# A mixing layer's output gate computed by tokens with seven half products, multiplied into the normalised mLSTM rows ahead of their transposes

## The chip, the cores and the metric

The kernel runs on one core of a Trainium2 chip. Its engines are TensorE (PE in the profile, with its weight loads listed apart as PEld), VectorE (DVE), ScalarE (ACT), GpSimd (POOL) and SyncE (SP, which here only issues DMAs). Each engine works through its own list of instructions in order and waits on semaphores for the others. The metric is device time of one execution in microseconds; the execution under the profiler has a time of its own.

## The reference

One decoder layer on 512 tokens of width 1024, all in float32. One RMS-normalised input `h` goes through one wide projection, of which this case touches two pieces of 1024 columns: `v_ml`, the values of the mLSTM (4 heads of 256), and `o_ml`, its output gate.

```python
h = rmsnorm(x, norm_mix_g[i])
proj = h @ w_in[i]
qk_ml, v_ml, o_ml, if_pre, q_sw, k_sw, v_sw, g_a, g_b = jnp.split(proj, split_idx, axis=-1)
...
h_ml = mlstm_chunkwise(q_ml, k_ml, v_ml.reshape(B, S, ML_HEADS, ML_DV), ig, lf)
h_ml = h_ml * lax.rsqrt(jnp.mean(h_ml * h_ml, axis=-1, keepdims=True) + EPS)
h_ml = h_ml.reshape(B, S, ML_V_W).astype(x.dtype) * mlstm_norm_g[i].astype(x.dtype)
y_a = jax.nn.sigmoid(o_ml) * h_ml
...
merged = jax.nn.sigmoid(g_a) * (y_a @ w_branch_a[i]) + jax.nn.sigmoid(g_b) * (y_b @ w_branch_b[i])
x = x + merged @ w_out[i]
```

`ig` and `lf` are an input gate and a log forget gate of each token and head (from `if_pre`), and `y_b` is sliding-window attention. An MLP, a gated embedding and a last norm follow; the change leaves them alone.

## The kernel before

A float32 product is made of three matmuls of a rounded kind: each operand is split into a high part (a cast, on ACT) and a low part (operand less high part, on DVE), and high·high, high·low and low·high are added in PSUM. `split` (lines 131 to 138) does it, `load_w` splits a weight tile of 128x1024, `pairs` lists the three. In the profile a weight's parts are `wh` and `wl`, those of the normalised input `h`. A tile of 128 by 512 results with the contraction over 1024 takes 24 matmuls of 512 columns.

The work in order: norm and transposes of the input; the values and gates of the attention (`vs`, `gt`); its keys (`kk`, `kl`, line 357 on); the output gate `w_o`; the mLSTM's scalar gates; the values `w_vml`; the branch gates `w_gb`, `w_ga`; the projections of queries and keys mixed with the attention; then, head by head, the mLSTM's rows beside the projection `w_b`; `w_a`; `w_out`; the MLP and the rest.

The output gate before. `o_proj(i)` computes eight tiles of 128 channels by 512 tokens (`proj_T`, the channels on the partitions), takes a sigmoid on ACT, and stores the tile in DRAM (`god`) by a DMA that POOL issues. Its eight calls are spread: two after the scalar gates' work, three after the sums of `h` (below), three after the transposes of the scalar gates. Much later `ya_of(h)` transposes the normalised rows of head `h`, multiplies them by the norm's gain and by the gate loaded back from `god` (line 825, tile `sy`), and splits the result into `ya`.

The values before. `vml` uses a scheme of seven half products in place of eight: tokens, contraction and columns are each cut in halves, and `seven` (line 488) forms sums of weight blocks on DVE (lines 497, 498, 503, 505) and products with parts of `h` and with sums `S1` to `S4` of parts of `h`. The sums `s1` to `s4` (line 449) and their splits (`hS`) are made once and serve the branch gates too. Each half product is 24 matmuls of 512 columns, four weight tiles' worth of two, and each goes to a pair of PSUM banks: X for `p1` and then `c11`, Z for `t21`, `t22`, `c12`, Y for `c22`, `c21`. `p1` is copied out of X by ACT (line 548) before the second product is added onto X; `t21` and `t22` are read out of Z by DVE (line 553) before the next product is added onto Z.

What sets the order. The kernel is written as one stream; a scheduling layer lays out a list for each engine, close to the written order with some instructions pulled ahead, and it may not change the order of two that depend on each other. `tc.issue_after` names an instruction behind which others must stand. Tiles come from pools with a fixed number of buffers: four each for `wh`, `wl` and raw weights `wr`, four `lm`, two `pT`, 34 of 128x512 (`act`), and in PSUM two each of `g`, `t` (one bank) and `a` (two banks).

Of the kernel before, what the change touches and what calls it, by code (L numbers as in the profile page):

```python
# [10 lines left out]
F32 = mybir.dt.float32  # L11
F32R = mybir.dt.float32r
AF = mybir.ActivationFunctionType
# [10 lines left out]
NH = 4  # L24
# [12 lines left out]
def block_kernel(  # L37
# [309 lines left out]
    def proj_T(wd, i, bank=ps_g):  # L347
        ps = bank()
        mm_T(ps, load_w(wd[i], KT * P, KT), hT)
        return ps  # L350
# [15 lines left out]
        kk.append(both)  # L366
        kl.append(low)


    dp = pool(ctx, "dp", space=bass.MemoryType.DRAM)  # L370
    god = [dp.tile([P, 2, 512], F32, name=nm("god")) for _ in range(4)]


    obanks = []

    def o_bank(i):
        if i in (0, 1, 6, 7):
            return ps_g()
        if i == 2:
            obanks.extend(four_a())  # L380
        return obanks[i - 2]

    def o_proj(i):
        ps = proj_T(w_o, i, lambda: o_bank(i))
        t = act_f("sgo")
        A.activation(t, ps, AF.Sigmoid)
        nc.gpsimd.dma_start(out=god[i // 2][:, i % 2, :], in_=t)


    pgi, pgf = ps_t(), ps_t()  # L390
    for m in range(NT):
        T.transpose(pgi[:4, m * P : (m + 1) * P], gt[:, m, :4], ident)
# [8 lines left out]
    A.activation(lf, lf, AF.Ln, bias=1.0)  # L401
    V.scalar_tensor_tensor(lf, fg, 0.0, lf, ALU.min, ALU.subtract)
    mst = act_f("mst")[:4, :]
    V.tensor_tensor_scan(mst, lf, ig, 0.0, ALU.add, ALU.max)
    fl = act_f("fl")[:4, :]
    for c in range(NT):
        V.tensor_tensor_scan(fl[:, c * P : (c + 1) * P], lf[:, c * P : (c + 1) * P], zeros4, 0.0, ALU.add, ALU.add)
    rr = act_f("rr")[:4, :]
    V.tensor_sub(rr, fl, mst)
# [12 lines left out]
    em = act_f("em")[:4, :]  # L422
    A.activation(em, mst, AF.Exp, scale=-1.0)
    o_proj(0)
    o_proj(1)


    hf[0] = tk("hf")[:, :D].rearrange("p (k c) -> p k c", k=KT)
# [37 lines left out]
    S3 = h_split(s3)  # L466
    S4 = h_split(s4)
# [20 lines left out]
    def seven(form, prod, X, Y, Z, b, post):  # L488


        b11, b12, b21, b22 = b
        n = range(len(b11))
        for i in n:
            prod(X, A11, form(b11[i]), i, True)
        post("p1", X)
        for i in n:
            V.tensor_sub(b12[i], b22[i], b12[i])
            V.tensor_add(b11[i], b12[i], b11[i])
        for i in n:
            prod(X, A12, form(b21[i]), i, False, True)  # L500
        post("c11", X)
        for i in n:
            V.tensor_sub(b21[i], b21[i], b11[i])
            prod(Z, S2, form(b11[i]), i, True)
            V.tensor_sub(b11[i], b22[i], b11[i])
        post("t21", Z)
        for i in n:
            prod(Z, S1, form(b11[i]), i, False)
        post("t22", Z)
        for i in n:  # L510
            prod(Y, S3, form(b12[i]), i, True)
        post("c22", Y)
        for i in n:
            prod(Z, S4, form(b22[i]), i, False, True)
        post("c12", Z)
        for i in n:
            prod(Y, A22, form(b21[i]), i, False, True)
        post("c21", Y)
# [5 lines left out]
        G.memset(t[:, :, DV : DV + 1], 1.0)  # L524
        vm.append(t)

    def vml():
        raws = quads(w_vml, ["wr", "wr", "lm", "lm", "wr", "wr", "lm", "lm"])
        a, b = ps_a(), ps_a()
        X, Y, Z = [a[:, :512], a[:, 512:]], [b[:, :512], b[:, 512:]], [ps_g(), ps_g()]  # L530
        keep = {}

        def prod(ps, f, w, kh, first, last=False):
            for t in range(2):
                ops = []
                for k in range(2):
                    ops += pairs([h[:, t * P : (t + 1) * P] for h in f[2 * kh + k]], [h[:, k, :] for h in w])
                chain(ps[t], ops, first and kh == 0, last and kh == 1, True)

        def post(what, ps):  # L540
            for t in range(2):
                if what[0] == "c":
                    half, nh = int(what[1]), int(what[2]) - 1
                    o = vm[t + (2 if half == 1 else 0)][:, 2 * nh : 2 * nh + 2, :DV]
                    src = ps[t].rearrange("p (h d) -> p h d", h=2)
                if what == "p1":
                    keep["p1", t] = act_f("p1")
                    A.copy(keep["p1", t], ps[t])
                elif what == "c11":
                    A.copy(o, src)  # L550
                elif what[0] == "t":
                    keep[what, t] = act_f(what)
                    V.tensor_add(keep[what, t], ps[t], keep["p1", t])
                else:
                    k = keep["p1" if what == "c12" else "t" + what[1:], t]
                    V.tensor_add(o, src, k.rearrange("p (h d) -> p h d", h=2))

        seven(lambda r: load_w(None, 1024, 2, r), prod, X, Y, Z, [raws[2 * i : 2 * i + 2] for i in range(4)], post)

    vml()  # L560

# [237 lines left out]
    def ml_norm(heads, rds):  # L799
        n = len(heads) * NT  # L800
        rs = rstd_of(hss[:, heads[0] : heads[-1] + 1, :].rearrange("p h t -> p (h t)"), DV)
        for j, h in enumerate(heads):
            V.tensor_mul(rs[:, j * NT : (j + 1) * NT], rs[:, j * NT : (j + 1) * NT], rds[j])
            for t in range(NT):
                V.tensor_scalar_mul(h_of(h, t), h_of(h, t), rs[:, j * NT + t : j * NT + t + 1])


    t2 = [None] * 8
# [9 lines left out]

    def ya_of(h):
        for i in (2 * h, 2 * h + 1):  # L820
            sg = act_f("sy")
            pt = ps_t()
            for t in range(NT):
                T.transpose(pt[:, t * P : (t + 1) * P], h_of(h, t)[:, (i % 2) * P : (i % 2 + 1) * P], ident)
            V.scalar_tensor_tensor(sg, pt, gml[:, i : i + 1], gate_of(god, i), ALU.mult, ALU.mult)
            split(ya[i], sg)

    ml_weights(0)
    rds = []
# [352 lines left out]
    return w.reshape(2, 2, 2, P, 2, 512).transpose(0, 2, 4, 3, 1, 5).reshape(8, P, 1024)  # L1182


def _heads(w):

    k = w.shape[0]
    return w.reshape(k, 2, 2, 4, 64).transpose(0, 1, 3, 2, 4).reshape(k, 1024)
# [6 lines left out]
def _layout(i):  # L1195
# [3 lines left out]
        "x": i["x"][0],  # L1199
        "p": i["p"][0, 0],  # L1200
        "w_qkml": _t_form(w[:, 0:1024]),
        "w_vml": _quarters(w[:, 1024:2048]).reshape(2, 4, P, 1024).transpose(1, 0, 2, 3).reshape(8, P, 1024),
# [41 lines left out]
```

## Time and profile before

| | |
|---|---|
| median of 3 runs | 906.15 us (904.98 to 906.18) |
| the profiled execution's own time | 905.84 us |
| its span, first to last instruction | 904.1 us |
| PE, DVE, ACT busy in the span | 890.4, 627.0, 466.9 us |
| from the first `w_o` matmul's stretch to the first branch gate's | 38.96 to 123.42 us |

A row of a time list reads: start, duration, engine, line, operation, out<-in, shapes, count, and in brackets the idle time of the engine before it and who ended it. Consecutive instructions of an engine overlap by their latency, so the cost of one in a row of many is the distance of starts. A row of waits reads: who waited, for whom, total us, times, longest. In a table by stretches each engine's busy time stands with its count of instructions.

### The profile page before, as it was taken

How to read it: one execution, taken by the hardware profiler on the slowest of the kernel's cores; microseconds unless marked ns; L12 is line 12 of the kernel's file. 1: busy time of each engine (PE TensorE's matmuls, PEld its weight loads, DVE VectorE, ACT ScalarE, POOL GpSimd, SP SyncE). 2: the span in 40 equal slices, each digit the busy share in tenths (PEclk: the TensorE clock that was granted, in tenths of full speed). 3: DMA queues.
4: the chain of work that ended last, by engine and by line, in shares of the span. 5: the costliest groups of instructions: out<-in, count | busy, mean ns of one | idle time of the engine just before them, and what ended most of it. 6: DMA issues, size and time to landing. Idle time of an engine off the chain costs nothing.

```text
span 904.1 us, 11781 instructions
## 1 busy us (share of the span) xinstructions
PE 890.4 (98%) x4500; PEld 741.6 (82%) x4500; DVE 627.0 (69%) x1016; ACT 466.9 (52%) x778; POOL 28.1 (3%) x47
## 2 busy tenths in 40 slices
PE   8999999999999999999999999999999999999996
PEld 7888899998877677777878888888888888888786
DVE  6884687874787977557644568856965795689556
ACT  6473444443676667664322555345535543554753
POOL 2021000000000000001210000000000000000000
PEclk9999999999999999999999999999999999999999
DMA  7753134435121132234452620631262044101402
GB/s 259 252 159 125 47 116 157 149 122 168 61 70 52 43 117 71 94 103 150 144 187 94 228 74 2 209 119 45 68 212 94 1 162 161 49 24 50 160 1 94
DMA packets 30347, 101.52 MB, mean 112 GB/s; under 512 B 4301, under 2 KB 4813, under 8 KB 30290
## 3 DMA queue, kind: packets, MB, share of 16 engines
q1 hardware_dynamic: 28002, 93.15, 31.0%
q0 software_dynamic: 2144, 7.35, 2.3%
q8 instruction: 35, 0.57, 0.3%
q10 hardware_dynamic: 144, 0.26, 0.1%
q14 instruction: 22, 0.18, 0.1%
HBM read 91.30 MB, written 8.40 MB: 110 GB/s over the span
## 4 chain that ended last, share of the span: by engine, by line
PE 73%; ACT 2%; DVE 2%; DMA 1%; issue 0%; SPq 0%; ACTq 0%
PE psg L162 42%; PE psp L162 22%; PE pst L784 2%; PE pst L713 1%; PE psa L705 1%; PE pst L774 1%; PE psa L162 1%; PE psa L668 1%; PE psa L669 1%; DMA gfin<-in_g_fin 1%; PE psp L877 1%; ACT jk L796 1%; ACT wh L134 1%; ACT pT L707 0%; DMA ptok<-in_p 0%
## 5 line engine op out<-in xcount | busy, mean ns | idle before, releaser
L135 DVE TENSOR_TENSOR wl<-wr,wh 128x1024 fp32r<-128x1024 f32 x134 | 170.7, 1279 | 131.0 <-ACT wh L134 124.4
L134 ACT CAST wh<-wr 128x1024 fp32r<-128x1024 f32 x134 | 140.9, 1053 | 208.5 <-PE psg L162 85.6
L162 PE MATMUL psg<-x,wh 128*128 128x512 f32 x512 | 157.9, 389 | 0.0
L162 PE MATMUL psp<-wh,uf 128*128 128x512 f32 x448 | 139.2, 390 | 0.0
L162 PEld LDWEIGHTS psg<-x,wh 128*128 128x128 f32 x512 | 96.0, 188 | 19.8
L162 PE MATMUL psg<-h,wh 128*128 128x512 f32 x320 | 101.3, 395 | 0.0
L162 PE MATMUL psg<-x,wl 128*128 128x512 f32 x256 | 99.6, 389 | 0.0
L162 PEld LDWEIGHTS psp<-wh,uf 128*128 128x128 f32 x448 | 84.1, 188 | 17.4
L162 PE MATMUL psp<-wl,uf 128*128 128x512 f32 x224 | 87.2, 390 | 0.0
L134 ACT CAST wh<-wd 128x1024 fp32r<-128x1024 f32 x44 | 46.3, 1055 | 60.4 <-PE psp L162 23.2
L162 PEld LDWEIGHTS psg<-h,wh 128*128 128x128 f32 x320 | 58.7, 188 | 15.9 <-issue 4.9
L135 DVE TENSOR_TENSOR wl<-wd,wh 128x1024 fp32r<-128x1024 f32 x44 | 53.3, 1220 | 17.6 <-ACT wh L134 17.4
L162 PE MATMUL psg<-h,wl 128*128 128x512 f32 x160 | 62.8, 393 | 0.0
L162 PEld LDWEIGHTS psg<-x,wl 128*128 128x128 f32 x256 | 48.1, 188 | 10.0
L162 PE MATMUL psa<-h,wh 128*128 128x256 f32 (+1 forms) x256 | 55.1, 311 | 0.2 <-ACT p L593 0.2
L162 PEld LDWEIGHTS psp<-wl,uf 128*128 128x128 f32 x224 | 42.0, 188 | 8.7
L135 DVE TENSOR_TENSOR uf<-F,uf 128x1792 fp32r<-128x1792 f32 (+2 forms) x20 | 33.0, 1652 | 21.8 <-ACT uf L134 21.8
L162 PEld LDWEIGHTS psa<-h,wh 128*128 128x128 f32 x256 | 41.8, 190 | 3.7 <-ACT p L593 0.9
L162 PE MATMUL psg<-yb,wh 128*128 128x512 f32 x128 | 42.7, 408 | 0.0
L162 PE MATMUL psg<-ya,wh 128*128 128x512 f32 x128 | 40.7, 394 | 0.0
L162 PE MATMUL psa<-h,wl 128*128 128x256 f32 (+1 forms) x128 | 39.6, 309 | 0.0
L134 ACT CAST uf<-F 128x1792 fp32r<-128x1792 f32 (+2 forms) x20 | 28.0, 1399 | 19.3 <-DVE F L951 19.2
(284 smaller groups left out, 1667.7 us busy)
## 6 DMA issues: line engine op xcount, KB each, us to landing
wr<-in_w_up SPq DMA_DIRECT2D x32, 512.0 KB, 3.2
wd<-in_w_down SPq DMA_DIRECT2D x24, 512.0 KB, 3.3
wr<-in_w_o SPq DMA_DIRECT2D x8, 512.0 KB, 4.8
gd<-gr POOLq DMA_DIRECT2D x8, 512.0 KB, 3.2
wr<-in_w_qsw SPq DMA_DIRECT2D x8, 512.0 KB, 4.0
wr<-in_w_qkml SPq DMA_DIRECT2D x8, 512.0 KB, 3.3
wr<-in_w_b SPq DMA_DIRECT2D x8, 512.0 KB, 3.2
gl<-gd SPq DMA_DIRECT2D x8, 512.0 KB, 3.4
```

Of the source, the lines that this page charges most:

```text
L134: A.copy(dst[0], src)
L135: V.tensor_sub(dst[1], src, r32(dst[0]))
L162: last_mm[0] = T.matmul(ps, l, r, start=first and i == 0, stop=last and i == len(ops) - 1, skip_group_check=parts)
L668: T.matmul(o, q[:, n * P : (n + 1) * P], kk[kp][ab][:, k0 : k0 + 256], start=True, stop=False)
L669: T.matmul(o, q[:, n * P : (n + 1) * P], kl[kp][ab][:, k0 : k0 + 256], start=False, stop=True)
L705: T.transpose(pt[:, c : c + P], lm3[ab][:, g, j * P : (j + 1) * P], ident)
L713: T.matmul(o[HALF[ab], :], vs[n + 1 - nk + j][:, c : c + 64], pTs[j][:, ab * 512 : (ab + 1) * 512], start=j == 0, stop=j == nk - 1,)
L774: T.matmul(psc[:, n0:], qk[4 + h][:, n0 : n0 + P], qk[h][:, n0:], start=True, stop=True)
L784: T.matmul(pn[:, : DV + 1], wT[s][:, t * P : (t + 1) * P], vm[s][:, h, :], start=s == 0, stop=s == t)
L796: A.activation(jk[:, :DV], h_of(h, t), AF.Square, scale=rd[:, t : t + 1], accum_out=hss[:, h, t : t + 1])
L877: T.transpose(ps[:, m * P : (m + 1) * P], xk[m][:, k * P : (k + 1) * P], ident)
```

## The change

The output gate is computed by tokens (tokens on the partitions), with `seven`, as the values are, and through the same code: `by_tokens(w, post)` is the old `vml`, and `post_by_tokens(done)` its old `post`. `w_vml` is computed first, directly behind the keys; the scalar gates' work follows; then `w_o`. The weights of `w_o` are laid out as those of `w_vml`. The gate's quarter results go through a sigmoid (`put_o`) to one DRAM tile `god` of tokens by heads. `ml_norm` loads a head's gate (`og`) and multiplies it into the normalised rows in the instruction that scaled them; `ya_of` transposes these rows and splits them, with the gain as scale, straight out of PSUM. The definitions and the work of `s1` to `s4` move ahead of the scalar gates. In the values' call alone the third product is placed behind the second (`own_first`).

```diff
-    def o_proj(i):
-        ps = proj_T(w_o, i, lambda: o_bank(i))
-        t = act_f("sgo")
-        A.activation(t, ps, AF.Sigmoid)
-        nc.gpsimd.dma_start(out=god[i // 2][:, i % 2, :], in_=t)
...
+    s1, s1h = h_sum("s1", hf_part(2, 1), hf_part(2, 2), ALU.add)
+    s2, s2h = h_sum("s2", s1h, hf_part(1, 1), ALU.subtract)
+    S2 = h_split(s2)
+    S1 = h_split(s1)
+    s4, _ = h_sum("s4", hf_part(1, 2), s2h, ALU.subtract)
+    s3, _ = h_sum("s3", hf_part(1, 1), hf_part(2, 1), ALU.subtract)
+    S3 = h_split(s3)
+    S4 = h_split(s4)
+
+    def seven(form, prod, X, Y, Z, b, post, own_first=False):
...
+        for i in n:
+            prod(X, A11, form(b11[i]), i, True)
+        post("p1", X)
+        for i in n:
+            V.tensor_sub(b12[i], b22[i], b12[i])
+            V.tensor_add(b11[i], b12[i], b11[i])
+        for i in n:
+            prod(X, A12, form(b21[i]), i, False, True)
+        own = last_mm[0].ins
+        post("c11", X)
+        for i in n:
+            V.tensor_sub(b21[i], b21[i], b11[i])
+            w = form(b11[i])
+            with tc.issue_after(own) if own_first else ExitStack():
+                prod(Z, S2, w, i, True)
+            V.tensor_sub(b11[i], b22[i], b11[i])
...
+    def post_by_tokens(done):
+
+        keep = {}
+
+        def post(what, ps):
+            for t in range(2):
+                if what == "p1":
+                    keep["p1", t] = act_f("p1")
+                    A.copy(keep["p1", t], ps[t])
+                elif what[0] == "t":
+                    keep[what, t] = act_f(what)
+                    V.tensor_add(keep[what, t], ps[t], keep["p1", t])
+                else:
+                    k = None if what == "c11" else keep["p1" if what == "c12" else "t" + what[1:], t]
+                    done(t + (2 if what[1] == "1" else 0), int(what[2]) - 1, ps[t], k)
...
+    by_tokens(w_vml, post_by_tokens(put_v), True)
 
     pgi, pgf = ps_t(), ps_t()
...
-    o_proj(0)
-    o_proj(1)
...
-    for i in range(2, 5):
-        o_proj(i)
...
-    for i in range(5, 8):
-        o_proj(i)
...
-    vml()
+    god = dp.tile([P, NH, NT, DV], F32, name="god")
+
+    def put_o(m, nh, ps, k):
+        if k is None:
+            k = act_f("sgo")
+            A.activation(k, ps, AF.Sigmoid)
+        else:
+            V.tensor_add(k, ps, k)
+            A.activation(k, k, AF.Sigmoid)
+        nc.gpsimd.dma_start(out=god[:, 2 * nh : 2 * nh + 2, m, :], in_=k.rearrange("p (h d) -> p h d", h=2))
+
+    by_tokens(w_o, post_by_tokens(put_o))
...
+            og = tok_scratch("og").rearrange("p (t d) -> p t d", t=NT)
+            nc.sync.dma_start(out=og, in_=god[:, h])
             for t in range(NT):
-                V.tensor_scalar_mul(h_of(h, t), h_of(h, t), rs[:, j * NT + t : j * NT + t + 1])
+                c = j * NT + t
+                V.scalar_tensor_tensor(h_of(h, t), h_of(h, t), rs[:, c : c + 1], og[:, t, :], ALU.mult, ALU.mult)
...
-            V.scalar_tensor_tensor(sg, pt, gml[:, i : i + 1], gate_of(god, i), ALU.mult, ALU.mult)
-            split(ya[i], sg)
+            split(ya[i], pt, gml[:, i : i + 1])
...
-        "w_o": _t_form(w[:, 2048:3072]),
+        "w_vml": _by_quarter(w[:, 1024:2048]),
+        "w_o": _by_quarter(w[:, 2048:3072]),
```

The first place is ACT where the values' first product is copied out. Before, at the start of `vml`, the casts of the sums (`hS`) lie far back, behind the first tiles of the output gate, and the copies stand between casts of weights:

```order
L386 ACTIVATE sgo_147_819<-psg_143_788 128x512
L134 CAST wh_177_940<-wr_162_874 128x1024
L386 ACTIVATE sgo_152_853<-psg_148_822 128x512
L134 CAST wh_179_959<-wr_157_864 128x1024
L548 COPY p1_173_916<-psa_165_880 128x512
L548 COPY p1_174_918<-psa_165_880 128x512
L134 CAST wh_181_977<-wr_158_866 128x1024
```

The same place in the change, ACT again; `psa_105` is X, `wh_119` and `wh_121` are weights of the third product, the names from `hS_75` to `hS_91` the high parts of `s2`, `s1`, `s3`, `s4`:

```order
L134 CAST wh_119_613<-wr_97_518 128x1024
L134 CAST hS_75_472<-s2_74_469 128x512
L134 CAST hS_77_476<-s2_74_469 128x512
L134 CAST wh_121_631<-wr_98_520 128x1024
L134 CAST hS_79_480<-s1_73_466 128x512
L134 CAST hS_81_484<-s1_73_466 128x512
L134 CAST hS_85_494<-s3_84_491 128x512
L134 CAST hS_87_498<-s3_84_491 128x512
L134 CAST hS_89_502<-s4_83_488 128x512
L134 CAST hS_91_506<-s4_83_488 128x512
L479 COPY p1_113_570<-psa_105_534 128x512
L479 COPY p1_114_572<-psa_105_534 128x512
```

All eight casts of the sums now stand ahead of the two copies of `p1`.

The second place is DVE, which makes the sums that those casts read. Before, `s4` and `s3` are made right behind the splits of `s2` and `s1`, with one weight's low part among them:

```order
L135 TENSOR_TENSOR hS_107_596<-s2_105_592,hS_106_595 128x512
L135 TENSOR_TENSOR wl_146_792<-wr_144_789,wh_145_791 128x1024
L135 TENSOR_TENSOR hS_109_600<-s2_105_592,hS_108_599 128x512
L135 TENSOR_TENSOR hS_111_604<-s1_104_589,hS_110_603 128x512
L135 TENSOR_TENSOR hS_113_608<-s1_104_589,hS_112_607 128x512
L449 TENSOR_TENSOR s4_114_611<-hf_43_265,s2_105_592 128x4x128
L449 TENSOR_TENSOR s4_114_611<-hf_51_318,s2_105_592 128x4x128
L449 TENSOR_TENSOR s3_115_614<-hf_43_265,hf_103_587 128x4x128
L449 TENSOR_TENSOR s3_115_614<-hf_51_318,hf_34_214 128x4x128
```

In the change, DVE at the same sums (lines 430 and 434 are differences of `w_vml`'s blocks):

```order
L135 TENSOR_TENSOR wl_120_614<-wr_97_518,wh_119_613 128x1024
L135 TENSOR_TENSOR hS_78_477<-s2_74_469,hS_77_476 128x512
L434 TENSOR_TENSOR wr_97_518<-wq_103_530,wr_97_518 128x1024
L135 TENSOR_TENSOR hS_80_481<-s1_73_466,hS_79_480 128x512
L430 TENSOR_TENSOR wr_102_528<-wr_102_528,wr_98_520 128x1024
L135 TENSOR_TENSOR hS_82_485<-s1_73_466,hS_81_484 128x512
L135 TENSOR_TENSOR wl_122_632<-wr_98_520,wh_121_631 128x1024
L393 TENSOR_TENSOR s4_83_488<-hf_43_265,s2_74_469 128x4x128
L393 TENSOR_TENSOR s4_83_488<-hf_51_318,s2_74_469 128x4x128
L434 TENSOR_TENSOR wr_98_520<-wq_104_532,wr_98_520 128x1024
L393 TENSOR_TENSOR s3_84_491<-hf_43_265,hf_72_464 128x4x128
L393 TENSOR_TENSOR s3_84_491<-hf_51_318,hf_34_214 128x4x128
```

Sums and splits of `w_vml`'s blocks, which before came after the output gate's tiles, now stand between and ahead of `s4` and `s3`.

The third place is PE at the transposes of the scalar gates (`gg`, `em`). Before, they stand behind a whole tile of the output gate (`psa_125`):

```order
L162 MATMUL psa_125_634<-h_16_158,wh_135_703 128x512
L162 MATMUL psa_125_634<-h_15_157,wl_136_704 128x512
L477 MATMUL pst_138_734<-ident_77,gg_88_506 128x4
L479 MATMUL pst_138_734<-ident_77,em_92_517 128x4
L477 MATMUL pst_138_734<-ident_77,gg_89_507 128x4 x2
```

In the change, on PE again, they stand in `w_o`'s first product (`psa_169` is its X; a name in brackets is an engine on whose count the row waits):

```order
L162 MATMUL psa_169_879<-wh_175_899,h_16_158 128x512
L540 MATMUL pst_160_841<-ident_77,gg_155_828 128x4 [waits DVE_49]
L162 MATMUL psa_169_879<-wh_175_899,h_15_157 128x512
L162 MATMUL psa_169_879<-wl_176_900,h_15_157 128x512
L162 MATMUL psa_169_879<-wh_175_899,h_16_158 128x512
L162 MATMUL psa_169_879<-wh_175_899,h_15_157 128x512
L162 MATMUL psa_169_879<-wl_176_900,h_15_157 128x512
L162 MATMUL psa_169_879<-wh_175_899,h_16_158 128x512
L542 MATMUL pst_160_841<-ident_77,em_159_839 128x4 [waits Activation_49]
```

So PE reaches for the scalar gates six matmuls before the first product of `w_o` is complete.

More of the change, by code (lines that the diff above doesn't have):

```diff
@@ L370, in block_kernel @@
     dp = pool(ctx, "dp", space=bass.MemoryType.DRAM)
[L371 to L381, printed above, removed]
-    def o_proj(i):
-        ps = proj_T(w_o, i, lambda: o_bank(i))
-        t = act_f("sgo")
-        A.activation(t, ps, AF.Sigmoid)
-        nc.gpsimd.dma_start(out=god[i // 2][:, i % 2, :], in_=t)
+    hf[0] = tk("hf")[:, :D].rearrange("p (k c) -> p k c", k=KT)
@@ new lines, in block_kernel, with h_part, hf_part, h_sum @@
+    with tc.issue_after(gate_in.ins):
+        hi, lo = [r32(t[:, :, :P]) for t in h2]
+        V.tensor_add(hf[0], hi, lo)
+    def h_part(tok, par):
+        o = 0 if tok == 2 else 256
+        return [[t[:, 2 * k + par - 1, o : o + 256] for t in h2] for k in range(4)]
+    def hf_part(tok, par):
+        return [hf[t + (2 if tok == 1 else 0)].rearrange("p (k two) c -> p k two c", two=2)[:, :, par - 1, :] for t in range(2)]
+    A11, A12, A22 = h_part(1, 1), h_part(1, 2), h_part(2, 2)
+    def h_sum(name, a, b, op):
+        t = sp.tile([P, 4, 256], F32, tag="pT", bufs=2, name=nm(name))
+        halves = [t[:, :, :P], t[:, :, P:]]
+        for i in range(2):
+            V.tensor_tensor(halves[i], a[i], b[i], op)
+        return t, halves
@@ new lines, in h_split @@
+    def h_split(t):
+        f = []
+        for kh in range(2):
+            hl = [q.rearrange("p (k c) -> p k c", k=2) for q in act_hl("hS")]
+            split(hl, t[:, 2 * kh : 2 * kh + 2, :])
+            f += [[q[:, k, :] for q in hl] for k in range(2)]
+        return f
+    s1, s1h = h_sum("s1", hf_part(2, 1), hf_part(2, 2), ALU.add)
[3 more added lines that the diff above has]
+    s4, _ = h_sum("s4", hf_part(1, 2), s2h, ALU.subtract)
@@ new lines, in block_kernel, with by_tokens, prod @@
+    vm = []
+    for m in range(NT):
+        t = tk("vm").rearrange("p (h d) -> p h d", h=NH)
+        G.memset(t[:, :, DV : DV + 1], 1.0)
+        vm.append(t)
+    def by_tokens(w, post, own_first=False):
+        raws = quads(w, ["wr", "wr", "lm", "lm", "wr", "wr", "lm", "lm"])
+        a, b = ps_a(), ps_a()
+        X, Y, Z = [a[:, :512], a[:, 512:]], [b[:, :512], b[:, 512:]], [ps_g(), ps_g()]
+        def prod(ps, f, w, kh, first, last=False):
+            for t in range(2):
+                ops = []
+                for k in range(2):
+                    ops += pairs([h[:, t * P : (t + 1) * P] for h in f[2 * kh + k]], [h[:, k, :] for h in w])
+                chain(ps[t], ops, first and kh == 0, last and kh == 1, True)
+        seven(lambda r: load_w(None, 1024, 2, r), prod, X, Y, Z, [raws[2 * i : 2 * i + 2] for i in range(4)], post, own_first)
@@ L521, in block_kernel @@
-    vm = []
-    for m in range(NT):
-        t = tk("vm").rearrange("p (h d) -> p h d", h=NH)
[L524 to L558, printed above, removed]
```

88 lines of the change are left out of this document (26 added, 62 removed).

## The prediction

> **What bounds the kernel now.** I read the page first: its rows of busy time and the slices.
>
> ```profile
> PE 890.4 (98%) x4500; PEld 741.6 (82%) x4500; DVE 627.0 (69%) x1016; ACT 466.9 (52%) x778; POOL 28.1 (3%) x47
> ...
> PE   8999999999999999999999999999999999999996
> DVE  6884687874787977557644568856965795689556
> ```
>
> PE is full in all slices but the first and the last; DVE reaches nine tenths in four. Then the list of who waits for whom, for PE over the whole span, tells whether that busy PE is held up by anything:
>
> ```profile
> PE psa L705 <- ACT pT L707: 1.6, 1, 1.6
> PE psp L877 <- DVE x L138: 1.1, 2, 0.6
> ...
> PE pst L824 <- DVE sy L825: 0.2, 1, 0.2
> PE pst L784 <- DVE hd L788: 0.2, 1, 0.2
> ```
>
> It is not: the longest wait in mid-run is 1.6 us. So the kernel is a stream of matmuls, a matmul fewer is time gained, and a wait put in front of PE is time lost unless PE is late anyway. The stretch that the change rewrites, from the keys' end to the first branch gate, comes from the table by stretches:
>
> ```profile
> 38.96:123.42 84.46, 84.41 (x384) 68.77 (x383) 57.07 (x74) 41.27 (x51) 7.48 (x17) 1.00 0.37 119
> ```
>
> In 84.46 us PE is never idle for long; DVE works 57.07 and ACT 41.27. What a matmul of 512 columns costs comes from the chain of work that ended last, where one tile stands whole:
>
> ```profile
> 235.99 5.47 PE psg L162 x24
> ```
>
> That is 0.228 us for each. The 192 of the output gate and 168 of the values make 82.1 us of the 84.46.
>
> **Fewer matmuls: 5.5 us.** The output gate goes from eight tiles of 24 to seven half products of 24. That takes 24 x 0.228 = 5.5 us off PE.
>
> **What the engines beside PE get.** Six more weight tiles are split (14 for 8), eight sums of weight blocks and ten additions out of PSUM come in. The prices are distances of starts in DVE's time list of before:
>
> ```profile
> 29.91 1.22 DVE L135 TENSOR_TENSOR wl<-wr,wh 128x1024 fp32r<-128x1024 f32 x1
> 31.04 1.22 DVE L431 TENSOR_TENSOR hf<-h,h 128x1024 f32<-128x1024 f32 x1
> 32.17 1.22 DVE L497 TENSOR_TENSOR wq<-wq,wq 128x1024 f32<-128x1024 f32 x1
> 33.31 0.68 DVE L449 TENSOR_TENSOR s<-hf 128x512 f32<-128x512 f32 x1
> 33.91 1.29 DVE L449 TENSOR_TENSOR s<-s,hf 128x512 f32<-128x512 f32 x2
> 35.12 0.68 DVE L363 TENSOR_TENSOR kl<-pst,kk 64x512 fp32r<-64x512 f32 x1
> ```
>
> An operation on 1024 elements costs 1.13 us, one on 512 costs 0.61. DVE gets 6 x 1.13 + 8 x 1.13 + 10 x 0.61 = 21.9 us: 79 us of work where it had 57. As an average that still fits under PE. But averages hide where the work stands, and by the order it stands in the worst place.
>
> **The values' first product: PE waits 13.2 us.** The second product is added onto X, so it cannot start before ACT has copied `p1` out of X. Before, this cost nothing: ACT stood idle waiting for PE, not PE for ACT.
>
> ```profile
> 90.61 1.08 ACT L548 COPY p<-psa 128x512 f32<-128x512 f32 x2 [1.62 <-PE psa L162]
> ...
> 63.57 2.19 ACT L134 CAST hS<-s 128x512 fp32r<-128x512 f32 x4 [0.68 <-DVE s L449]
> 65.66 0.59 ACT L386 ACTIVATE sgo<-psa 128x512 f32<-128x512 f32 x1
> ```
>
> In the change the two copies stand behind all eight casts of sums, and ACT is in order. The casts of `s3` and `s4` wait for DVE to make them. Up to the row of 29.91 DVE has the same list as before. From there to the last half of `s3` stand fourteen operations on 1024 (`hf`, five low parts of weights, eight sums and differences of `w_vml`'s blocks) and fifteen on 512 (four of the keys' `kl`, seven halves of sums, four splits): 14 x 1.13 + 15 x 0.61 = 25.0, so `s3` is complete at 54.9 to 55.0. I find nothing that DVE would wait for in between, nor anything that lets it be quicker: its weights are issued no later than those that stood in their places. Then ACT: four casts 2.1 us (63.57 to 65.66 above), two copies 1.08, hand-overs some 0.2: done at 58.3.
>
> PE would be ready long before. It ends the keys and starts the first product where this row stands:
>
> ```profile
> 38.96 0.60 PE L392 MATMUL pst<-ident,gt 128*4 128x128 f32 x4
> 39.32 0.71 PE L162 MATMUL psg<-h,wh 128*128 128x512 f32 x2
> ```
>
> 38.96 + 5.47 for 24 matmuls + 0.7 for eight transposes of `gt` (0.36 for four, between the two rows) = 45.1. Nothing else of PE's may go ahead: its list is in order, and the third product stands behind the second. The wait is 58.3 - 45.1 = 13.2 us. Bounds: none of the DVE prices can shrink, since they are distances in a full engine; a hand-over of 0.1 at each of a dozen crossings would add 1.2. So 13.0 to 14.4, and I take 13.2, the sum of the rows.
>
> **The pace after so long a wait: 2.0 us.** At the start of the run matmuls go at half pace:
>
> ```profile
> 11.30 0.59 PE L162 MATMUL psg<-wl,h 128*128 128x264 f32 x1 [0.96 <-DVE wl L319]
> 11.69 0.64 PE L162 MATMUL psg<-wh,h 128*128 128x264 f32 x2
> ...
> 12.35 0.64 PE L162 MATMUL psg<-wh,h 128*128 128x264 f32 x2
> ...
> 15.38 0.53 PE L162 MATMUL psg<-wh,h 128*128 128x264 f32 x2
> 15.74 0.28 PE L162 MATMUL psg<-wl,h 128*128 128x264 f32 x1
> 15.86 0.41 PE L162 MATMUL psg<-wh,h 128*128 128x264 f32 x2
> ...
> 16.23 0.41 PE L162 MATMUL psg<-wh,h 128*128 128x264 f32 x2
> ```
>
> Three take 0.66 us from 11.69 to 12.35 and 0.37 from 15.86 to 16.23. Full pace comes about 4.1 us after PE began to work without a break at 11.30. The granted clock doesn't show this, it is 1.00 in both:
>
> ```profile
> 12.00:14.00 2.00, 2.00 (x11) 2.00 (x11) 1.97 (x4) 1.97 (x4) 0.00 (x0) 1.00 0.87 261
> 16.00:18.00 2.00, 1.76 (x15) 1.55 (x14) 1.55 (x5) 1.28 (x4) 0.00 (x0) 1.00 1.06 256
> ```
>
> No row of before shows PE after an idle of 13 us; the nearest are the start, and the 1.6 us wait, which is too short to tell. Bounds: 0, if the pace stays, and 5.5, if the whole second product runs at half pace. I take half of the 4.1 us, 2.0, from the start's rows. The Trainium skill's page "TensorE: Matmul & The Clock Gate" (Part 1, the clock gate) speaks against this change: by it the array falls to half its clock after an idle window of about 3.4 us and needs such a window of work to return. By that rule an estimate is 1.7 us lost, half of that window, and 915.7 in the end; the start's rows agree with it in kind, at 4.1 us.
>
> **The scalar gates in `w_o`'s first product: 1.1 us.** I leave the slow pace out of the clock times here, since it shifts all of them alike. From 58.3 six products of 5.47 follow each other and end the values at 91.1; DVE reads `t21` and `t22` out of Z in time there, since DVE has by then made all it could ahead. Then PE does 18 matmuls of `w_o` (to 95.2) and wants the first transpose of `gg`, which DVE makes at the end of this chain:
>
> ```profile
> 50.53 0.68 DVE L402 SCALAR_TENSOR_TENSOR lf<-fg,lf 4x512 f32<-4x512 f32 x1 [2.66 <-ACT lf L401]
> 51.24 1.21 DVE L404 TENSOR_TENSOR_SCAN mst<-lf,ig 4x512 f32<-4x512 f32 x1
> 52.38 1.33 DVE L407 TENSOR_TENSOR_SCAN fl<-lf,zeros 4x128 f32<-4x128 f32 x4
> 53.75 0.68 DVE L409 TENSOR_TENSOR rr<-fl,mst 4x512 f32<-4x512 f32 x1
> ```
>
> DVE enters it late. The low part of the last weight of the values stands ahead, and its buffers come free when PE ends the fourth product after the wait, at 80.2 (58.3 + 4 x 5.47); cast, two additions and hand-overs put it at 82.2. From there DVE has six operations on 1024 (6.8), seven on 512 (4.3), the two scans 1.14 + 1.3, and 0.5 for the logarithm on ACT: 96.3 us. PE waits about 1.1 us. Bounds: 0; and 3.4, if the two weights whose difference stands in DVE's list just before take 5.5 us to land, like `w_vml`'s, and not 3.2, like the branch gates':
>
> ```profile
> wr<-in_w_gb SPq DMA_DIRECT2D x6, 512.0 KB, 3.2
> ...
> wr<-in_w_vml SPq DMA_DIRECT2D x4, 512.0 KB, 5.5
> ```
>
> Their transposes cost PE 1 us, as before. The copies of `w_o`'s `p1` are then done within 0.3 us of PE asking.
>
> **Queues.** SP's loads of `w_o` now stand behind two of `w_gb`, which wait for `s3` and `s4` to be split, and each waits for a buffer of `w_vml`; the first lands near 66, twenty microseconds ahead of its use; the pair just priced is the one without margin. POOL has the `vm` memsets, then the scalar gates' DMAs, then the eight `god` stores; its results are read 200 us later. ACT gets six more casts and two copies, some 7 us on 41. The branch gates then start in the same relation to DVE as before.
>
> **The rows' end: 0.** In `ml_norm` sixteen multiplications get a second operand, in `ya_of` eight multiplications on 512 go, and the low part is made from PSUM. The rows:
>
> ```profile
> 411.71 1.14 DVE L805 TENSOR_SCALAR hs<-hs,rs 128x256 f32<-128x256 f32 x4
> 412.76 0.69 DVE L814 TENSOR_TENSOR gb<-psg,gl 128x512 f32<-128x512 f32 x1
> 413.36 1.40 DVE L825 SCALAR_TENSOR_TENSOR sy<-pst,gml,gl 128x512 f32<-128x512 f32 x2
> ```
>
> DVE saves 8 x 0.66 and pays 16 x 0.1, by half of a 512 row against 0.26. PE waited 0.2 us there twice, so at most 0.4 is gained; a PSUM buffer held until DVE's low part is made may cost up to 1. I take 0. The four `og` loads take the place of four loads of the gate.
>
> **The sum.** New stretch: 336 x 0.228 = 76.6, transposes 0.7 + 1.0, waits 13.2 + 1.1, slow pace 2.0: 94.6 for 84.46, so 10.1 us more. Everything after it is PE's stream and moves as a whole. On the profiled execution's 905.84 us that is 916.0; it stands 0.3 below the median of 906.15, which I don't add. From no change about 0.2% can be told here, by the spread of the three runs.
>
> **Rivals.** (a) As summed: 916.0. (b) The wait comes, the pace stays: 914.0. For it: the clock column never moves; against it: the start's rows. (c) More is late: the loads' 2.3, the whole second product slow (3.5 more), or the rows' end: 918 to 921. For it: DVE works 79 us in 94.6 with everything in order. (d) Faster: ACT reaches the `p1` copies when PE is done. Then 905.84 - 5.5 + 1.1 = 901.4. It decides at one place: as soon as the copies end before 49.5, 4.4 us after PE asks, the matmuls saved outweigh both waits. Against it: DVE would have to make `s3` by 46.2 instead of 55, eight operations on 1024 fewer. (e) DVE is ahead by some, and the wait is 6 to 10 us: 907 to 912.
>
> **Chances.** (a) 0.45, (b) 0.23, (c) 0.20, (d) 0.04, (e) 0.08. Between the ends of (b) less the rows' gain and most of (c), 912.5 to 920.5, lie (a), (b) and most of (c): 0.83. Slower 0.95, faster 0.04, the same 0.01.
>
> **What would show it.** In the profile after: a wait of PE of some 13 us at about 45, put down to the copy of `p1` on ACT (line 479), ACT at the casts of `hS` until 57, DVE without a gap from 30 to 55; matmuls at 0.45 us for some 4 us behind it; a wait of about 1 us at line 540; the first branch gate's matmul at 133.5 instead of 123.42, and from there a constant shift. The prediction is wrong if ACT takes the copies earlier than its list says, or if DVE's operations are cheaper in this mix.

## The result, and the profile after

| | before | after |
|---|---|---|
| median of the runs | 905.63 us (4 runs, 904.98 to 906.18) | 917.47 us (4 runs, 917.04 to 920.20) |
| the profiled execution | 905.84 us, span 904.1 | 917.04 us, span 915.3 |

The change makes the kernel slower: the ratio is 1.0137, with a 95% interval of 1.0125 to 1.0149. The page of the profile after, its busy time and slices:

```profile
PE 887.0 (97%) x4476; PEld 738.7 (81%) x4476; DVE 646.5 (71%) x1032; ACT 474.3 (52%) x786; POOL 28.6 (3%) x47
...
PE   8949999999999999999999999999999999999997
...
PEclk9979999999999999999999999999999999999999
```

PE has its 24 matmuls less (x4476 for x4500) and a hole in the third slice, where the granted clock (the row PEclk, in tenths of full speed) falls to seven tenths as well. Who waits for whom, PE over the whole span:

```profile
PE psa L162 <- ACT p L479: 13.4, 1, 13.4
PE psg L162 <- DVE wl L319: 1.6, 1, 1.6
PE psa L705 <- ACT pT L707: 1.6, 1, 1.6
PE pst L540 <- DVE gg L529: 1.1, 1, 1.1
```

The first and the last are new. The other two stood there before, at 1.0 and 1.6. The time lists of the three engines around the long wait, DVE, ACT and PE in turn:

```profile
54.87 1.28 DVE L393 TENSOR_TENSOR s<-hf,hf 128x512 f32<-128x512 f32 x2
56.84 2.50 DVE L135 TENSOR_TENSOR hS<-s,hS 128x512 fp32r<-128x512 f32 x4 [0.68 <-ACT hS L134]
```

```profile
46.26 1.13 ACT L134 CAST hS<-s 128x512 fp32r<-128x512 f32 x2
56.19 2.18 ACT L134 CAST hS<-s 128x512 fp32r<-128x512 f32 x4 [8.80 <-DVE s L393]
58.40 1.07 ACT L479 COPY p<-psa 128x512 f32<-128x512 f32 x2
```

```profile
45.81 0.27 PE L503 MATMUL pst<-ident,gt 128*4 128x128 f32 x1
59.52 0.80 PE L162 MATMUL psa<-wh,h 128*128 128x512 f32 x1 [13.44 <-ACT p L479]
...
61.40 0.63 PE L162 MATMUL psa<-wl,h 128*128 128x512 f32 x1
...
62.68 0.63 PE L162 MATMUL psa<-wl,h 128*128 128x512 f32 x1
...
67.65 0.39 PE L162 MATMUL psg<-wh,hS 128*128 128x512 f32 x1
...
135.90 0.40 PE L162 MATMUL psa<-h,wh 128*128 128x256 f32 x2
```

The chain reads from the back: PE waits for the copies of `p1`, these stand behind four casts on ACT, ACT has waited 8.8 us for `s3`, and DVE ends `s3` at 56.15 without a gap ahead of it. Behind the wait three matmuls take 1.28 us (61.40 to 62.68), and the second product ends 8.13 us after its start (59.52 to 67.65). The last row is the first branch gate, 12.48 us later than before. By the table of stretches the clock is halved from inside the wait until 65.0 (the column behind POOL's):

```profile
47.94:51.35 3.41, 0.00 (x0) 0.00 (x0) 3.41 (x5) 0.00 (x0) 0.00 (x0) 1.00 0.00 0
51.35:58.17 6.82, 0.00 (x0) 0.00 (x0) 6.14 (x10) 1.98 (x4) 0.32 (x4) 0.50 0.00 0
58.17:61.58 3.41, 2.06 (x5) 1.68 (x6) 1.17 (x2) 1.27 (x3) 0.00 (x0) 0.50 0.62 184
61.58:64.99 3.41, 3.41 (x10) 2.64 (x9) 0.00 (x0) 0.00 (x0) 0.00 (x0) 0.50 0.33 124
64.99:68.40 3.41, 3.41 (x17) 2.80 (x16) 1.22 (x1) 1.60 (x3) 0.00 (x0) 1.00 0.00 0
```

Two marks in the chain that ended last divide the rest: the first transposes of w_out and the last projection. Before, and then after:

```profile
482.39 0.44 PE psp L877 x4
...
873.96 23.27 PE psg L162 x192
```

```profile
494.41 0.44 PE psp L878 x4
...
885.17 23.26 PE psg L162 x192
```

| place | before | after | difference |
|---|---|---|---|
| end of the keys, where the stretch starts | 38.96 | 39.61 | +0.65 |
| from there to the first branch gate | 84.46 | 96.29 | +11.83 |
| from there to w_out's transposes | 358.97 | 358.51 | -0.46 |
| from there to the last projection | 391.57 | 390.76 | -0.81 |

Together 11.21, as the marks at the end (885.17 for 873.96) and the spans (915.3 for 904.1) have it. The first and the last lines differ from execution to execution: over the kernels below the start lies between 38.63 and 39.49 and the last stretch between 390.72 and 391.99, though nothing was edited there.

### The profile page after: what moved, and what is told of

The parts are those of the page before. It is cut to its first block, busy times and chain, and to the rows that moved or that the text cites. A ratio compares the mean times of both kernels' runs of the same rounds, so it can differ in the third digit from the quotient of the medians.

```text
span 915.3 us, 11761 instructions
## 1 busy us (share of the span) xinstructions
PE 887.0 (97%) x4476; PEld 738.7 (81%) x4476; DVE 646.5 (71%) x1032; ACT 474.3 (52%) x786; POOL 28.6 (3%) x47
## 4 chain that ended last, share of the span: by engine, by line
PE 74%; ACT 2%; DVE 1%; DMA 1%; issue 0%; ACTq 0%
PE psg L162 42%; PE psp L162 23%; PE pst L784 2%; PE pst L713 1%; PE psa L705 1%; PE pst L774 1%; PE psa L162 1%; PE psa L668 1%; PE psa L669 1%; DMA gfin<-in_g_fin 1%; PE psp L878 1%; ACT wh L134 0%; PE pst L826 0%; ACT pT L707 0%; ACT jk L796 0%
## 5 line engine op out<-in xcount | busy, mean ns | idle before, releaser
L135 DVE TENSOR_TENSOR wl<-wr,wh 128x1024 fp32r<-128x1024 f32 x136 | 173.9, 1283 | 122.2 <-ACT wh L134 122.1
L134 ACT CAST wh<-wr 128x1024 fp32r<-128x1024 f32 x136 | 142.8, 1051 | 198.7 <-PE psg L162 84.5
L162 PE MATMUL psg<-h,wh 128*128 128x512 f32 x256 | 81.4, 396 | 0.0
L162 PEld LDWEIGHTS psg<-h,wh 128*128 128x128 f32 x256 | 46.9, 188 | 13.5 <-issue 4.9
L162 PE MATMUL psg<-h,wl 128*128 128x512 f32 x128 | 50.3, 393 | 0.0
L162 PE MATMUL psa<-wh,h 128*128 128x512 f32 x96 | 32.7, 413 | 13.4 <-ACT p L479 13.4
L976 DVE SCALAR_TENSOR_TENSOR xk<-psp,r,xk 128x512 f32<-128x512 f32 x48 | 33.8, 745 | 3.5 <-PE psp L162 3.2
L162 PE MATMUL psg<-hS,wh 128*128 128x256 f32 x192 | 35.6, 284 | 0.0
```

The source lines that it names most:

```text
L134: A.copy(dst[0], src)
L135: V.tensor_sub(dst[1], src, r32(dst[0]))
L162: last_mm[0] = T.matmul(ps, l, r, start=first and i == 0, stop=last and i == len(ops) - 1, skip_group_check=parts)
L976: pin(V.scalar_tensor_tensor(o, ps[:, t, :], r2[:, 2 * toks + t : 2 * toks + t + 1], o, ALU.mult, ALU.add))
```

## The experiments

Theory A is that of the prediction: PE loses the time by waiting for the copies, then by the pace behind so long a wait, then at the scalar gates. Theory B is that DVE's added work bounds the whole stretch, so that a wait removed comes back at a later product. Theory C is that the matmuls behind the wait are slow for another reason than the wait.

The fill edits, third_first and late_sums are made to the changed kernel; p1_first builds on late_sums, gates_later on p1_first, and the last two on gates_later.

**fill_wait: matmuls put into the wait.**

```diff
         post("p1", X)
+        if own_first:
+            after_p1 = last_mm[0].ins
+            for j in range(54):
+                with tc.issue_after(after_p1):
+                    after_p1 = T.matmul(Z[0], A11[0][0][:, :P], h2[0][:, 0, :], start=True, stop=True).ins
...
-            prod(X, A12, form(b21[i]), i, False, True)
+            w = form(b21[i])
+            with tc.issue_after(after_p1) if own_first else ExitStack():
+                prod(X, A12, w, i, False, True)
```

> The changed kernel with 54 extra matmuls of 512 columns (on the rows of h, into the bank that the third product overwrites) between the values' first and second products: 54 x 0.228 = 12.3 us of work inside the 13.4 us wait. The engines beside PE keep their order. Theory A (matmuls are slow after the wait because PE stood idle): PE has no long idle, the second product takes 5.5 us for 8.13, the time falls by 2.7 to 914.8. Theory C (they are slow for another reason, such as what ACT and DVE do in that moment, or the bank that was just copied): the second product still takes 8.1 us and the time stays at 917.5.

Measured 914.46 us (914.12 to 915.02), ratio 1.0098 (1.0083 to 1.0113). Doing 54 matmuls more, the kernel is 3.0 us faster than the changed one. PE's time list:

```profile
44.52 12.40 PE L426 MATMUL psg<-h 128*128 128x512 f32 x54
...
59.00 0.50 PE L162 MATMUL psa<-wh,h 128*128 128x512 f32 x1 [1.21 <-ACT p L488]
...
64.58 0.39 PE L162 MATMUL psg<-wh,hS 128*128 128x512 f32 x1
```

The second product takes 5.58 us for 8.13. It reads the same bank behind the same copies, with ACT and DVE in the same order; so C falls, and the idle is the cause.

**fill_half and fill_most: 27 and 48 matmuls for 54** (the diff is that of the first).

```diff
-            for j in range(54):
+            for j in range(27):
```

> As fill_wait with 27 extra matmuls in place of 54: PE stands idle for about 7.3 us, 52 to 59. Theory A by the length of an idle (anything of several us lets the pace fall): the second product is slow again, 8.1 us, and the time is that of the changed kernel, 917.5. If the loss grows in step with the idle: half of it, 1.4 us, 916.1. Theory C: as with any number of extra matmuls, 8.1 us.

> As fill_wait with 48 extra matmuls: PE stands idle for about 2.6 us, the length of the wait after which late_sums showed slow matmuls (2.45), and longer than the 1.2 of fill_wait, after which there were none. If the idle's length alone decides: slow matmuls for some 3.4 us again, 1.7 to 2.7 us lost, 916 to 917.5. If the pace falls only when an idle fills some fixed stretch of time, it may fall or not: 914.5 or 916.

fill_half gave 916.03 us, fill_most 913.89; these are single runs, so what follows rests on the traces. In fill_half PE stands idle for 7.30 us and the second product runs at half clock until 62.69:

```profile
52.45:55.86 3.41, 0.00 (x0) 0.00 (x0) 3.02 (x5) 0.35 (x1) 0.32 (x4) 1.00 0.00 0
55.86:59.28 3.42, 0.44 (x1) 0.45 (x2) 2.49 (x4) 2.90 (x6) 0.00 (x0) 0.50 0.24 50
59.28:62.69 3.41, 3.41 (x9) 2.64 (x9) 0.00 (x0) 0.00 (x0) 0.00 (x0) 0.50 0.73 257
```

It starts at 58.84, so 3.85 us are slow where the changed kernel had 5.47 (59.52 to 64.99). At half clock half of such time is lost: 1.9 for 2.7, and the stretch to the branch gates is 95.51 for 96.29. The 916.1 that I gave for a loss in step with the idle is met for another reason: what counts is when the clock comes back. In fill_most, after 2.54 us of idle (56.49 to 59.03), no matmul is slow at all. The stretches of 3.41 us in which the clock is low lie on one grid throughout a run (see the last section). At the start of this run the clock is low from 12.87 to 16.28; eleven and twelve steps of 3.413 later lie 53.83 and 57.24:

```profile
12.87:16.28 3.41, 3.31 (x16) 3.04 (x16) 2.44 (x4) 2.55 (x7) 0.00 (x0) 0.50 0.83 256
53.83:57.24 3.41, 2.66 (x16) 1.80 (x15) 2.73 (x5) 1.54 (x3) 0.32 (x4) 1.00 0.00 0
57.24:60.65 3.41, 1.62 (x7) 1.36 (x8) 1.61 (x3) 1.71 (x4) 0.00 (x0) 1.00 0.55 167
```

So the edge at 57.24 cuts the idle into 0.75 and 1.79 us, and PE works for 1.62 us or more in each stretch. In late_sums (below) an idle of 2.45 lies but for 0.1 within one stretch, PE works for 1.06 us of that stretch, and the clock falls.

**third_first: the third product may go ahead of the second.**

```diff
-    by_tokens(w_vml, post_by_tokens(put_v), True)
+    by_tokens(w_vml, post_by_tokens(put_v))
```

> The changed kernel without the rule that the values' second product is issued ahead of the third: PE then has the third product (24 matmuls, 5.5 us), which needs no copy of p1, ahead of the second. The copies stay where they are, behind all eight casts of sums. Theory A: PE works about 5.5 us inside the former 13.4 us wait, in two halves at 48 and 53 us as their weights' low parts come; the time falls by 5.5 and, if shorter idles leave the pace alone, by up to 2.7 more: 909.3 to 912.0. A wait of PE for the copies of p1 of 3 to 4 us remains at 55 us. Theory B (DVE's added work is the bound of the whole stretch, wherever PE waits): the waits appear again at the scalar gates and in w_o's products, and the time stays above 914.

Measured 916.08 us (914.76 to 918.03), ratio 1.0117 (1.0102 to 1.0132): only 1.4 less than the change, far from A's 909 to 912. The waits of PE from 35 to 140 us, in the profiled execution (914.76, the fastest of its four), and the clock:

```profile
PE psa L162 <- ACT p L479: 5.1, 2, 4.4
PE psg L162 <- DVE wl L135: 3.1, 2, 2.2
PE pst L540 <- DVE gg L529: 1.5, 1, 1.5
PE pst L542 <- ACT em L533: 1.3, 1, 1.3
```

```profile
49.86:53.27 3.41, 1.22 (x6) 0.75 (x5) 3.41 (x5) 1.02 (x1) 0.00 (x0) 1.00 0.00 0
53.27:56.68 3.41, 3.04 (x8) 1.84 (x6) 3.41 (x5) 0.28 (x1) 0.31 (x4) 0.50 0.00 0
56.68:60.09 3.41, 0.00 (x0) 0.00 (x0) 2.43 (x4) 3.39 (x7) 0.00 (x0) 1.00 0.44 156
60.09:63.50 3.41, 2.83 (x7) 2.25 (x8) 2.82 (x5) 0.53 (x2) 0.00 (x0) 0.50 0.71 265
63.50:66.91 3.41, 3.41 (x17) 2.80 (x16) 0.80 (x1) 1.05 (x1) 0.00 (x0) 1.00 0.51 196
```

The wait of 13.4 is cut to three of 0.9, 2.2 and 4.4, as A said: 6.0 less. But three shorter waits lower the clock twice, so the pace costs as much as before: 3.04 and 2.83 us of work at half clock, 2.9 lost for 2.7. And at the scalar gates and in w_o PE now waits 1.5, 1.3 and 0.7 where it had waited 1.1: DVE and ACT are no earlier than they were. Here B is right for 2.4 us, and its mark, a time above 914, is met. The stretch to the branch gates is 93.48 us, 2.8 below that of the changed kernel.

**late_sums: `s4` and `s3` behind the third product.**

```diff
-    s4, _ = h_sum("s4", hf_part(1, 2), s2h, ALU.subtract)
...
-    S4 = h_split(s4)
+    S34 = []
+
+    def s_late():
+        if not S34:
+            s4, _ = h_sum("s4", hf_part(1, 2), s2h, ALU.subtract)
+            s3, _ = h_sum("s3", hf_part(1, 1), hf_part(2, 1), ALU.subtract)
+            S34.extend([h_split(s3), h_split(s4)])
+        return S34
...
         post("t21", Z)
+        S3, S4 = s_late()
```

> The changed kernel with s4 and s3 and their splits emitted behind the values' third product, so that ACT's copies of p1 stand behind four casts of sums (s2, s1), not eight; nothing else is moved by hand. Theory A: ACT copies p1 from 47.4 to 48.5 us, the wait falls from 13.4 to about 2.8, the slow pace (2.7) goes with it: 917.5 - 10.6 - 2.7 = 904.2, up to 906 if DVE, now without slack, makes PE wait 1 to 2 us at the scalar gates or in w_o's first products. Theory B (DVE's 22 us of added work bounds the stretch): the 13 us only move to later products, 913 or more.

Measured 908.18 us (906.91 to 911.39 in 10 runs), ratio 1.0034 (1.0023 to 1.0046). The long wait is 2.45 us, as A expected, and 9.3 us come back; B's 913 is out. But 2.2 more than A allowed are missing. The clock fell all the same:

```profile
45.21:48.62 3.41, 1.06 (x5) 0.89 (x6) 3.41 (x5) 2.27 (x5) 0.00 (x0) 1.00 0.00 1
48.62:52.03 3.41, 3.41 (x10) 2.63 (x9) 3.41 (x5) 0.00 (x0) 0.00 (x0) 0.50 0.00 0
```

The clock is full again from 52.03. That is 1.7 lost. PE had been back at work for a microsecond, at full pace, when the clock was halved. Waits of 0.6 for `t21`, 0.6 for `gg`, 1.3 for `em` and 0.7 in w_o are the rest.

**p1_first: the casts of `s1` behind the copies too.**

```diff
-    S1 = h_split(s1)
+    S1 = []
...
         post("c11", X)
+        if not S1:
+            S1.extend(h_split(s1))
```

> As late_sums, and the casts of s1 also behind the copies of p1: ACT copies p1 as soon as PE has ended the first product. Theory A: the wait falls to the two copies themselves and the hand-over, about 1.3 us, and the time to 902.7, up to 905 with DVE's lateness in w_o; this is faster than before (905.6). Theory B: as for late_sums, 913 or more, no faster than late_sums.

Measured 904.80 us (902.56 to 907.04 in 10 runs), ratio 0.9991 (0.9978 to 1.0003). It is within A's range, 12.7 us below the change with the same matmuls and nearly the same work on every engine, so the order is what cost the time. Faster than before it is not shown to be. ACT's row for the copies, the waits from 35 to 140 us, and the clock at the scalar gates:

```profile
45.94 1.07 ACT L486 COPY p<-psa 128x512 f32<-128x512 f32 x2
```

```profile
PE psa L162 <- ACT p L486: 1.4, 1, 1.4
PE psa L162 <- DVE wl L135: 1.0, 1, 1.0
PE pst L547 <- DVE gg L536: 0.9, 1, 0.9
PE psg L162 <- DVE t L489: 0.6, 1, 0.6
```

```profile
87.21:90.62 3.41, 2.37 (x19) 1.52 (x18) 3.15 (x9) 2.92 (x4) 2.17 (x4) 1.00 0.16 46
90.62:94.03 3.41, 3.41 (x9) 2.65 (x10) 3.41 (x4) 0.38 (x1) 0.00 (x0) 0.50 0.74 264
```

Four waits of 0.6 to 1.4 us, 3.9 in all, and 1.7 us of pace eat what the 24 matmuls save. From 44 to 98 us DVE has no gap of more than 0.7 us: it is late for everything by a little.

**gates_later: the scalar gates behind the branch gates.** The block from `pgi, pgf = ps_t(), ps_t()` to the copies of `gc` is moved as it is:

```diff
     gbd = gate_proj(w_gb)
     gad = gate_proj(w_ga)
+
+    pgi, pgf = ps_t(), ps_t()
...
```

> As p1_first, and the scalar gates (their transposes, the scans and gg on DVE, em on ACT) are emitted behind the branch gates' projections, at about 210 us, instead of between the values and w_o. In p1_first they cost PE a wait of 0.9 for gg, then one of 1.0 for a weight's low part that DVE made late, and then 3.4 us of matmuls at half pace, 1.7 lost. Theory A (what is left of the loss is DVE's lateness around the scalar gates): these 3.6 us go, the wait for the copies grows by the 0.9 us of transposes that stood ahead of it: 904.8 - 2.7 = 902.1, which is 905.6 less the 5.5 us of matmuls saved plus some 2 us of short waits. Theory B (DVE's work as a whole is the bound): the waits move on into w_o's products and the time stays within 1 us of 904.8.

Measured 904.20 us (903.26 to 906.49 in 12 runs), ratio 0.9987 (0.9979 to 0.9996). The stretch to the branch gates is now 80.33 us, 4.1 below that of before, with the clock at 1.00 throughout; the only waits left in it are 1.4, 0.6 and 0.3. But the next stretch, to w_out, grows from 358.97 to 361.55: the transposes are paid there, and the wait for `gg` comes again at 207 us, 0.95. So A's 902.1 is missed by 2.1: it took the wait for `gg` as gone, and the wait came along. The 0.9 that A added is not there either: PE's list still has the transposes of `gt` ahead of the copies' wait (44.41 to 45.45), which stays at 1.4. Of the rest, by the profiles of p1_first and gates_later, 0.9 stands in the last stretch, which the edit doesn't touch, and something under a microsecond in the stretch to w_out; it was not traced further.

**gates_sums_later: `s4` and `s3` one product later still.**

```diff
         post("t21", Z)
-        S3, S4 = s_late()
...
         post("t22", Z)
+        S3, S4 = s_late()
```

> As gates_later, with s4 and s3 emitted behind the fourth product and not the third, so that DVE's addition of t21, for which PE waited 0.6 us in p1_first, is less late. Theory A: 0.6 us or less below gates_later, 901.5 to 902. Theory B: no gain, or a new wait for the splits of s3 ahead of the fifth product.

Measured 908.22 us (906.23 to 910.14 in 12 runs), ratio 1.0025 (1.0016 to 1.0035). The gain isn't there and the wait that I gave to theory B is:

```profile
PE psa L162 <- ACT hS L134: 1.7, 1, 1.7
...
PE psg L162 <- DVE t L489: 1.0, 1, 1.0
...
PE psa L162 <- DVE hS L135: 0.6, 1, 0.6
```

The fifth product waits for the splits of `s3`, and the clock is halved from 67.4 to 70.8 behind it. The wait for `t21` even grew, from 0.6 to 1.0. These 1.7, 0.6 and 0.4 us and 1.4 of pace make up the 4.0 us by which the kernel is slower than gates_later.

**transposes_apart: as gates_later, the transposes of `gg` and `em` 14 us behind DVE's work.**

```diff
     for i in range(4):
         q_proj(i)
 
+    pgc = ps_t()
...
```

> As gates_later, but the transposes of gg and em (and the copies of gc) stand behind the first four tiles of the sliding window's queries, some 14 us behind the scalar gates' work on DVE. In gates_later PE waited 0.95 us for gg at 207 us. Theory A (a short wait of PE is lost time wherever it stands, and goes when its maker is given time): 904.2 - 0.95 = 903.2. Rival: DVE's or ACT's other work there takes the place of the wait, and the time stays at 904.2.

Measured 905.04 us (903.60 to 906.75 in 11 runs), ratio 0.9997 (0.9988 to 1.0006). The rival was right. PE no longer waits for `gg`, and waits 0.9 and 0.4 for the queries on DVE instead:

```profile
PE psg L162 <- DVE qs L626: 0.9, 1, 0.9
...
PE psa L677 <- DVE qs L626: 0.4, 1, 0.4
```

The stretch to the branch gates, which the edit doesn't touch, took 81.31 us in this profile for 80.33, with a wait for a weight in w_o of 1.2 and not 0.3; so a microsecond between two profiles tells nothing by itself. The next stretch, which holds the edit, took 361.98 us for 361.55, so nothing was gained there either. gates_later has the lowest time of the series, 0.13% below the kernel before, though its interval overlaps those of p1_first and this kernel; of the 5.5 us of matmuls 1.3 are left.

## Why the prediction was right, and where it was off

- **Fewer matmuls, 5.5 us.** The trace has 24 fewer, and they cost 0.227 us each at full clock. The work that DVE gets was priced well too: it is busy for 77.91 us of the stretch, for 79.
- **The values' first product, 13.2 us.** Measured 13.4. The mechanism is shown, since p1_first changes nothing but where `s3`, `s4` and the splits of the sums stand, and the wait falls to 1.4. The stretch began 0.65 later. `s3` came at 56.15 for 54.9 to 55.0 and PE was ready at 46.1 for 45.1: beyond the common 0.65, DVE's list took some 0.6 longer and PE's work ahead of the wait 0.3, and these two partly cancel.
- **The pace after so long a wait, 2.0 us.** The mechanism is shown by fill_wait; the term was too small, 2.7. It was half of the start's 4.1 us of slow rows, and that is no measure of it: what is lost depends on when the clock returns, 2.7 here, 1.9 in fill_half, 1.7 in late_sums. The remark under rival (b), that the clock column never moves, was wrong for this wait: it shows 0.50. The Trainium skill's page "TensorE: Matmul & The Clock Gate" (Part 1) says that activity is judged in free-running windows of about 3.4 us and that one busy window brings the clock back. The rows of 3.41 us agree, with two limits: the window before a fall need not be idle (PE worked for 1.06 of 3.41 us in late_sums), and the one that ends it need not be full (2.83 of 3.41 in third_first). The estimate of 1.7 that I drew from that page left out the part of a window in which PE restarts, which stays slow as well (58.17 to 61.58 above).
- **The scalar gates in `w_o`'s first product, 1.1 us.** Measured 1.09, at the place and for the reason named, but the exact match is luck. PE asked at 99.40, 4.2 later than in the sum (95.2), which leaves the slow pace out. The low part of the values' last weight was done at 87.22, a microsecond later than 82.2 with that shift, and five operations on 1024 elements followed it ahead of `gg` where the sum had six; the two errors cancel.
- **The sum.** The stretch took 96.29 us for 94.6: 0.2 in the wait, 0.7 in the pace, and the remaining 0.8 in transposes, which cost 2.1 and not 1.7, and in hand-overs that the sum didn't have.
- **The rows' end, 0.** Measured -0.46 here; over the seven profiles that have the new rows' end and the scalar gates in their old place, the stretch from the branch gates to w_out is 358.39 to 358.84, mean 358.59, for 358.97: a gain of some 0.4. That is the end of the range that the prediction named; of the kernel before there is only the one profile.
- **Not foreseen:** the start (+0.65) and the loads near the end (-0.81), which differ between executions anyway and nearly cancel. With them the profiled run came to 917.04 for 916.0.
- **Rival (d)** was mispriced. p1_first does what it describes, the copies end at 47.0, and the time is 904.8, not 901.4; in late_sums they end at 47.5, before its deciding point of 49.5, and the kernel is slower than before. The rival kept only the wait at the scalar gates. In truth DVE, once PE no longer stands still, is late for `t21` and for a weight of w_o as well, the copies themselves take 1.4, and the small waits bring the clock down with them.

## What to carry to other kernels

Where PE is full, saving matmuls by sums on another engine can move the bound to the order of the queues beside PE, as here: look for an evacuation of PSUM that stands in order behind work which PE doesn't need yet, and put it ahead. Where a wait of PE reaches some two microseconds, or several of one stand close together, allow for slow matmuls on top: 1.4 to 2.7 us were lost here each time the clock fell, and none in fill_most, where it did not. Cutting the wait into pieces did not save the pace in third_first. And a saving priced on the bound engine alone holds only as far as the others have slack: of 5.5 us saved here, 1.3 remained in the best order tried.

## What the runs showed of the hardware

- The granted clock falls and returns on a grid (its edges are read off stretches of half a microsecond). In third_first it changes at 53.27, 56.68, 60.09 and 63.50, each 3.41 us apart; in the changed kernel it is low for 13.64, four times 3.41, in fill_half for 6.83, in late_sums and p1_first for 3.41. The grid holds through a run: in fill_most the clock returns at 16.28 and falls again at 907.16, near the end, 261 steps of 3.413 later. The changes don't begin with the idle: in late_sums the clock falls 1.06 us after PE resumed.
- A stretch need not be idle throughout. The clock fell after stretches in which PE was busy for 1.06 of 3.41 us (late_sums), 1.22 (third_first), 1.67 (gates_sums_later, 63.98 to 67.39) and 2.37, where 13 of the 19 matmuls are transposes of four columns (p1_first). Where an idle lies in the grid matters: 2.45 us, nearly all within one stretch, brought the clock down in late_sums, 2.54 cut by an edge did not in fill_most. But PE's busy time is not the whole measure, since the clock stayed after 1.56 (changed kernel, 44.52 to 47.93) and 1.62 (fill_most, 57.24 to 60.65). What exactly is counted stays open.
- The clock came back after stretches in which PE was busy throughout, and also after 3.04 and 2.83 us of 3.41 (third_first). After 2.06 (changed kernel, 58.17 to 61.58) it stayed low.
- At the start of the profile of before the clock column stands at 1.00 while matmuls go at half pace; after the change the column shows 0.50 from 13.80 to 17.21 us, and there three matmuls take 0.66 us (from 16.00) where three behind it take 0.37 (from 17.28). So the column of one profile can miss it.
- The runs of late_sums, p1_first and gates_sums_later, which have several waits of one to three microseconds, spread over 4.5, 4.5 and 3.9 us; those of the kernel before beside them, over 2.5 and 2.8. In gates_sums_later the six executions up to 907.74 us have a mean granted clock of 0.998 or 0.999 and the six from 908.70 on 0.994 to 0.997, which fits falls of the clock in some executions and not in others; in p1_first time and clock part less clearly (907.04 at 0.997, 903.84 at 0.995). That the clock's grid makes the spread is not shown.
